# Low parts of streamed weights: a negated write on ScalarE and an accumulating DMA in place of a subtraction on VectorE

## The chip, the cores and the metric

The kernel runs on one core of one Trainium2 chip. The core has a matrix engine (TensorE, PE in the profile), a vector engine (VectorE, DVE), a scalar engine (ScalarE, ACT), GpSimd (POOL), a queue engine that issues DMAs (SyncE, SP), and 16 DMA engines that all queues share. The metric is the device time of one execution in microseconds. Two runs of the kernel before took 730.09 and 731.26 us; the median is 730.67 us.

## The reference

One layer of a diffusion backbone on 512 latent tokens and 256 context tokens, width 1024, all in float32. What is computed, cut to the core:

```python
h  = _rmsnorm(x, pre_g) * (1.0 + sc) + sh           # modulated by silu(c) @ w_mod
hc = _rmsnorm(ctx, pre_g) * (1.0 + sc_c) + sh_c
b_gate, c_gate, x_in, z_a, q, k, v, z_b, g_a, g_b = _split_in(h @ w_in)   # ten blocks of 1024
q, k = _apply_rope(q), _apply_rope(k)
k_c, v_c = jnp.split(hc @ w_in[:, K_OFF:V_END], 2, axis=-1)
attn = _neighbourhood_attention(q, k, v, k_c, v_c, rpb)   # 8 x 16 window + all context keys, 16 heads
y_a = (jax.nn.silu(z_a) * b_gate * _dwconv3(c_gate * x_in, conv_w, conv_b)) @ w_out_conv
y_b = (jax.nn.silu(z_b) * attn) @ w_out_attn
merged = jax.nn.sigmoid(g_a) * y_a + jax.nn.sigmoid(g_b) * y_b
out = x + gt * _rmsnorm(merged @ w_o, post_g)
```

## The kernel before

**Products in three passes.** The matrix engine is used with the type fp32r, which keeps fewer digits than float32. To come close to float32, every operand X is kept as two tiles: a high part H, which is X rounded to fp32r, and a low part L = X - H. A product of weights w and moving data m is then the sum of three matmuls: w.H m.H, w.H m.L and w.L m.H (`step_T`, lines 112 to 117, in this order for every k). A low part is made by `split` (lines 67 to 76): ScalarE copies the source into H (line 70), VectorE subtracts H from the source (line 71).

**Streamed weights.** Most weights of `w_in` and both output weights pass through SBUF in chunks of 1 MB: 128 partitions x 8 k-blocks x 256 columns. `Chunk.__init__` allocates two raw tiles of 4 k-blocks each and has SP load them (line 84), 512 KB each. `Chunk.split` allocates one tile `w` that holds H and L of all 8 k-blocks side by side (in each k-block 256 columns of H, then 256 of L) and splits one half after the other. Raw tiles have 2 buffers, `w` has 2. So the raw load of a chunk can go out when the split of the chunk before has read its raw tiles, and the split of chunk n+1 can begin when PE has finished with chunk n-1, that is, when it begins chunk n. There are 45 streamed chunks. `Chunks` (lines 96 to 110) hands them out in the order of the list `order` and starts the load and split of the next one at each call.

**Stages.** The opening (to about 52 us) normalises x, computes the modulation on VectorE from `w_mod`, and multiplies the first three chunks' worth of weights in an order written out by hand (`manual_schedule` over PE, DVE, ACT and SP; GpSimd isn't among them). The first streamed chunk, `order[3]`, is loaded and split within it (lines 407 and 411). From about 52 to 107 us PE works on the last convolution units of the opening and on channels 2 and 3, chunk after chunk, while VectorE and ScalarE modulate the context tokens (`modulate_c`, which loads `w_mod` slabs through the same SP queue, lines 251 and 451). From 107 to 137 us come the first keys and queries and the first values. From 137 to 512 us attention runs in 64 blocks, with projections of the remaining chunks placed between them by the list `plan`; a block's softmax goes from PE through DVE, ACT, DVE, to PE's transposes, is split into TH and TL (lines 580 to 586) and multiplied with the values in `gather` (line 600). From 512 to 656 us the merge stage takes the output weights and the last gates, chunk after chunk (line 711 on). The end multiplies by `w_o`, whose weights are split by `load_wo` and not by `Chunk`.

**Order of the work.** Each engine runs its own list of instructions in order. In the opening the lists follow the program text. Elsewhere the framework's planner orders them when the kernel is built, by priority in program order and by the costs that it assumes; all semaphores come from the framework as well. PE's list follows the text closely, those of ACT and DVE are interleaved more.

**Where values are used.** In the projections with tokens moving (`unit`, lines 229 to 232) PE first needs a low part of a chunk at its third matmul, and the second half's at k = 4. In `proj_N` (line 128, for the values) one matmul streams H and L together, so the low part is needed at the first.

Of the kernel before, what the change touches and what calls it, by code (L numbers as in the profile page):

```python
# [12 lines left out]
ALU = mybir.AluOpType  # L13
# [14 lines left out]
def layer(ctx: ExitStack, tc, xp, ctxt, ctxT, cc, wmod, small, wfirst, win, wout, wo, rel, tab, out):  # L28
    nc = tc.nc
# [7 lines left out]
    class Banks:  # L37


        def __init__(self, *tags):  # L40
            self.tags, self.n = tags, 0
# [25 lines left out]
    def split(H, L, src, scale=None):  # L67

        if scale is None:
            nc.scalar.copy(H, src)  # L70
            nc.vector.tensor_sub(L, src, H.bitcast(F32))  # L71
        else:
            nc.scalar.mul(H, src, scale)
            nc.vector.scalar_tensor_tensor(
                out=L, in0=src, scalar=scale, in1=H.bitcast(F32), op0=ALU.mult, op1=ALU.subtract
            )

    class Chunk:


        def __init__(self, src):
            self.raws = [wp.tile([P, 4, 256], F32, name="raw", bufs=2) for _ in range(2)]
            for i, raw in enumerate(self.raws):
                nc.sync.dma_start(raw, src[:, 4 * i:4 * i + 4])

        def split(self):
            both = wp.tile([P, KT, 2, 256], F32R, name="w", bufs=2)
            for i, raw in enumerate(self.raws):
                s = slice(4 * i, 4 * i + 4)
                split(both[:, s, 0], both[:, s, 1], raw)  # L90
            return both[:, :, 0], both[:, :, 1], both

    def load_chunk(src):
# [141 lines left out]
    with ExitStack() as p0:  # L235
# [31 lines left out]
        def modulate(k, v, m, H, L):  # L267
            col = cols.pop((k, v))
            nc.scalar.activation(m, m, AF.Identity, bias=col[:, 1:2], scale=col[:, 0:1])
            split(H, L, m)  # L270
# [44 lines left out]
        with tc.manual_schedule(engines={E.PE, E.DVE, E.Activation, E.SP}):  # L315
# [74 lines left out]
            for k in range(KT):  # L390
                cast_first(k)
                condition(k, 0, [1])
                col = cols.pop((k, 0))
                nc.vector.tensor_mul(col[:, 0:1], col[:, 0:1], sp[:, PG + k:PG + k + 1])
                rest_first(k)
                if k == KT - 1:
                    nc.vector.tensor_scalar(out=hcv, in0=sp[:, CW:CW + 32], scalar1=0.5, scalar2=None, op0=ALU.mult)
                if k + 1 < KT:
                    condition(k + 1, 0, [0])
                m = st.tile([P, S], F32, name="m", bufs=2)  # L400
                nc.scalar.activation(m, turned_x.pop(k), AF.Identity, bias=col[:, 1:2], scale=col[:, 0:1])
                split(hx[0][k], hx[1][k], m)
                if k + 3 < KT:
                    load_slab(k + 3)
                    load_first(k + 3)
                elif k == 5:
                    after = Chunk(order[3])
                steps(k)
                if k + 2 < KT:
                    turned_x[k + 2] = turn_x(k + 2)  # L410
# [83 lines left out]
    def values(g):  # L494
        w = chunk()
        for p in (2 * g, 2 * g + 1):
            V[p] = aw.tile([P, 6, 2, P], F32R, name="V", bufs=3)
        for t in range(6):
            ps = pj()
            n = t % 4  # L500
            proj_N(ps, w, hx if t < 4 else hc, slice(n * P, (n + 1) * P))
            vs = summed(ps)
            for i, p in enumerate((2 * g, 2 * g + 1)):
                src = vs[:, i * P:(i + 1) * P].rearrange("p (h d) -> p h d", h=2)
                split(V[p][:, t, :, 0:64], V[p][:, t, :, 64:P], src)
            if t % 2:
                yield
# [371 lines left out]
```

## Time and profile before

| what | value |
|---|---|
| median of two runs | 730.67 us (730.09 to 731.26) |
| profiled execution, span from first to last instruction | 728.6 us; the page gives no other time for it |
| PE busy, instructions | 717.5 us (98%), 3512 matmuls |
| DVE busy | 515.1 us (71%) |
| ACT busy | 332.0 us (46%) |
| POOL busy | 0.7 us, 6 instructions |
| HBM read, written | 83.93 MB, 2.10 MB |
| mean granted TensorE clock | 0.998 |

Busy time is the share of the span in which an engine executes something; a line number such as L117 is that of the kernel. A group is a set of instructions of one line, engine and operation. A wait is the idle time of an engine together with what ended it. The chain is the work that ended last, followed back from the end. A DMA issue is named by its destination and source, with its queue; "SPq" is SP's queue.

### The profile page before, as it was taken

How to read it: one execution, taken by the hardware profiler on the slowest of the kernel's cores; microseconds unless marked ns; L12 is line 12 of the kernel's file. 1: busy time of each engine (PE TensorE's matmuls, PEld its weight loads, DVE VectorE, ACT ScalarE, POOL GpSimd, SP SyncE). 2: the span in 40 equal slices, each digit the busy share in tenths (PEclk: the TensorE clock that was granted, in tenths of full speed). 3: DMA queues.
4: the chain of work that ended last, by engine and by line, in shares of the span. 5: the costliest groups of instructions: out<-in, count | busy, mean ns of one | idle time of the engine just before them, and what ended most of it. 6: DMA issues, size and time to landing. Idle time of an engine off the chain costs nothing.

```text
span 728.6 us, 9358 instructions
## 1 busy us (share of the span) xinstructions
PE 717.5 (98%) x3512; PEld 602.6 (83%) x3512; DVE 515.1 (71%) x1060; ACT 332.0 (46%) x619; POOL 0.7 (0%) x6
## 2 busy tenths in 40 slices
PE   7999999999999999999999999999999999999996
PEld 4888888888888888888888888888888888888885
DVE  6979989996998968879879779675844324335323
ACT  6564523663464654555536446434823213314221
POOL 0000000000000000000000000000000000000000
PEclk9999999999999999999999999999999999999999
DMA  8985883213212222121322212322133133235402
GB/s 332 406 319 174 301 293 112 86 68 108 69 63 73 72 74 73 58 88 58 116 72 73 73 58 73 98 77 72 58 115 109 65 116 101 73 116 180 166 10 107
DMA packets 25967, 86.63 MB, mean 119 GB/s; under 512 B 3009, under 2 KB 3393, under 8 KB 25922
## 3 DMA queue, kind: packets, MB, share of 16 engines
q1 hardware_dynamic: 25778, 85.84, 34.2%
q8 instruction: 27, 0.44, 0.2%
q10 hardware_dynamic: 144, 0.20, 0.1%
q14 instruction: 18, 0.15, 0.1%
HBM read 83.93 MB, written 2.10 MB: 118 GB/s over the span
## 4 chain that ended last, share of the span: by engine, by line
PE 96%; DMA 1%; DVE 1%; ACT 1%; SPq 0%; issue 0%; DVEq 0%; ACTq 0%
PE ps L117 20%; PE ps L116 20%; PE ps L115 20%; PE ps L128 6%; PE ps L755 6%; PE ps L600 4%; PE ps L584 4%; PE ps L133 3%; PE ps L552 3%; PE ps L141 2%; PE ps L307 2%; PE ps L311 2%; PE ps L308 2%; DMA fraw<-in_wfirst 1%; PE ps L561 1%; PE ps L146 1%
## 5 line engine op out<-in xcount | busy, mean ns | idle before, releaser
L115 PE MATMUL ps<-h,w 128*128 128x512 f32 x528 | 207.5, 393 | 0.0
L117 PE MATMUL ps<-h,w 128*128 128x512 f32 x528 | 206.0, 390 | 0.0
L116 PE MATMUL ps<-h,w 128*128 128x512 f32 x528 | 205.7, 390 | 0.0
L71 DVE TENSOR_TENSOR w<-raw,w 128x1024 fp32r<-128x1024 f32 (+1 forms) x98 | 113.1, 1173 | 60.3 <-ACT w L70 60.1
L70 ACT CAST w<-raw 128x1024 fp32r<-128x1024 f32 (+1 forms) x98 | 97.0, 1016 | 95.2 <-PE ps L117 64.0
L117 PEld LDWEIGHTS ps<-h,w 128*128 128x128 f32 x528 | 99.1, 188 | 20.9
L116 PEld LDWEIGHTS ps<-h,w 128*128 128x128 f32 x528 | 99.2, 188 | 20.3
L115 PEld LDWEIGHTS ps<-h,w 128*128 128x128 f32 x528 | 99.2, 188 | 20.1
L575 ACT ACTIVATE pt<-ps,m 128x512 f32<-128x512 f32 x64 | 44.3, 694 | 60.2 <-DVE m L572 60.2
L568 DVE CUSTOM_DVE_ANT_1 ps<-ps,bt 128x512 f32<-128x512 f32 x56 | 38.6, 700 | 15.1 <-PE ps L552 12.0
L71 DVE TENSOR_TENSOR TL<-ps,TH 128x512 fp32r<-128x512 f32 x64 | 42.7, 679 | 5.2 <-ACT TH L70 5.2
L715 DVE SCALAR_TENSOR_TENSOR g<-g,ps 128x512 f32<-128x512 f32 x16 | 11.0, 686 | 42.4 <-PE ps L117 42.4
L70 ACT CAST TH<-ps 128x512 fp32r<-128x512 f32 x64 | 35.1, 588 | 6.6 <-PE ps L584 6.4
L633 ACT ACTIVATE g<-ps 128x512 f32<-128x512 f32 x16 | 9.6, 598 | 59.6 <-PE ps L117 59.6
L584 PE MATMUL ps<-ident,pt 128*128 128x128 f32 x256 | 33.3, 272 | 0.0
L128 PE MATMUL ps<-w,h 128*128 128x512 f32 x128 | 32.7, 395 | 0.0
L577 DVE TENSOR_SCALAR pt<-pt,z 128x512 f32<-128x512 f32 x64 | 30.8, 482 | 1.0
L584 PEld LDWEIGHTS ps<-ident,pt 128*128 128x128 f32 x256 | 29.4, 140 | 2.3
L600 PE MATMUL ps<-TH,V 128*128 128x256 f32 (+1 forms) x96 | 28.5, 319 | 0.0
L600 PE MATMUL ps<-TL,V 128*128 128x256 f32 (+1 forms) x96 | 27.7, 318 | 0.0
L128 PEld LDWEIGHTS ps<-w,h 128*128 128x128 f32 x128 | 23.1, 189 | 4.3
L517 ACT ACTIVATE qd<-ta 64x512 fp32r<-64x512 f32 x32 | 20.2, 631 | 13.5 <-PE ps L561 6.8
(158 smaller groups left out, 1134.9 us busy)
## 6 DMA issues: line engine op xcount, KB each, us to landing
raw<-in_win SPq DMA_DIRECT2D x74, 512.0 KB, 4.2
wm<-in_wmod SPq DMA_DIRECT2D x34, 512.0 KB, 7.2
raw<-in_wout SPq DMA_DIRECT2D x16, 512.0 KB, 4.1
bt<-in_rel SPq DMA_DIRECT2D x16, 256.0 KB, 2.6
raw<-in_wo SPq DMA_DIRECT2D x8, 512.0 KB, 4.2
fraw<-in_wfirst SPq DMA_DIRECT2D x8, 384.0 KB, 8.4
x<-in_xp SPq DMA_DIRECT2D x4, 512.0 KB, 5.4
xr<-in_xp SPq DMA_DIRECT2D x4, 512.0 KB, 5.9
```

The lines of the kernel that those rows point to most:

```text
L70: nc.scalar.copy(H, src)
L71: nc.vector.tensor_sub(L, src, H.bitcast(F32))
L115: nc.tensor.matmul(ps, lhsT=H[:, k, cs], rhs=mH[k], start=k == 0, stop=False)
L116: nc.tensor.matmul(ps, lhsT=H[:, k, cs], rhs=mL[k], start=False, stop=False)
L117: nc.tensor.matmul(ps, lhsT=L[:, k, cs], rhs=mH[k], start=False, stop=k == KT - 1)
L128: nc.tensor.matmul(ps, lhsT=mH[k][:, ts], rhs=both[:, k].rearrange("p a c -> p (a c)"), start=k == 0, stop=False, skip_group_check=True,)
L568: nc.vector.tensor_tensor_reduce(out=s3, in0=s3, in1=bt[:, e::4 - e][:, 0:2], scale=1.0, scalar=-3.0e38, op0=ALU.add, op1=ALU.max, accum_o ...
L575: nc.scalar.activation(pt, s, AF.Exp, bias=m, scale=1.0, accum_out=z)
L577: nc.vector.tensor_scalar(out=pt, in0=pt, scalar1=z, scalar2=None, op0=ALU.mult)
L584: nc.tensor.transpose(tp[:, c], pt[:, c * P:(c + 1) * P], ident)
L600: nc.tensor.matmul(o3[:, dst], lhsT=V[p][:, kt, h], rhs=src(t), start=n == 0 and t is TH, stop=n == len(work) - 1 and t is TL,)
L755: nc.tensor.matmul(ps, lhsT=mm[m][k][:, ts], rhs=w[k][:, cols], start=k + o == 0, stop=k == KT - 1 and o == 2)
```

## The change

Only `Chunk` is changed. For each half of a chunk ScalarE makes H as before, then writes the rounded weights a second time, negated, to the place of L: the product of the raw tile and -1, rounded to the type of the tile, is -H. Then a DMA issued by GpSimd reads the same raw weights once more from HBM and adds them to what lies there, so that the place holds raw - H. It has to wait for the negated write, and PE has to wait for it. VectorE has no part in it any more. The raw tiles are now read by ScalarE alone, twice. `split` itself stays for all other tiles (tokens, softmax tiles, values, merged data, `w_o`).

```diff
@@ -79,6 +79,7 @@
         def __init__(self, src):
+            self.src = src
             self.raws = [wp.tile([P, 4, 256], F32, name="raw", bufs=2) for _ in range(2)]
             for i, raw in enumerate(self.raws):
                 nc.sync.dma_start(raw, src[:, 4 * i:4 * i + 4])
@@ -87,7 +88,9 @@
             both = wp.tile([P, KT, 2, 256], F32R, name="w", bufs=2)
             for i, raw in enumerate(self.raws):
                 s = slice(4 * i, 4 * i + 4)
-                split(both[:, s, 0], both[:, s, 1], raw)
+                nc.scalar.copy(both[:, s, 0], raw)
+                nc.scalar.mul(both[:, s, 1], raw, -1.0)
+                nc.gpsimd.dma_start(both[:, s, 1], self.src[:, s], accum_op=ALU.add)
             return both[:, :, 0], both[:, :, 1], both
```

## The prediction

> **What bounds the kernel now.** I read the page's busy times and its chain first, then the waits of PE alone.
>
> ```profile
> PE 717.5 (98%) x3512; PEld 602.6 (83%) x3512; DVE 515.1 (71%) x1060; ACT 332.0 (46%) x619; POOL 0.7 (0%) x6
> ...
> PE 96%; DMA 1%; DVE 1%; ACT 1%; SPq 0%; issue 0%; DVEq 0%; ACTq 0%
> ```
>
> ```profile
> core 0 of [0], span 728.6 us
> engine line waited for: us in total, times, longest us
> PE ps L355 <- ACT crow L327: 3.3, 1, 3.3
> PE ps L307 <- ACT h L70: 1.1, 1, 1.1
> PE ps L552 <- ACT pt L575: 0.4, 1, 0.4
> ```
>
> PE is busy for 717.5 us of 728.6 and makes up 96% of the chain. A busy PE could still hide stalls, so the second view decides: PE waited three times, 4.8 us together, and the two longest come before any streamed weight is used (L355 and L307 belong to the opening). Whatever the change takes from VectorE, PE has at most 4.8 us to give back. The question is only whether the new way of making the low parts keeps PE free of waits.
>
> The profiled execution has a span of 728.6 us, 2.1 below the median of 730.67; I sum against the span and add 2.1.
>
> **What is removed and added.** A chunk is 1 MB of raw weights in two halves; 45 chunks make 90 halves.
>
> ```profile
> L70 ACT CAST w<-raw x98: 614/1051/1071, 45.1 to 687.6; 128x1024 fp32r<-128x1024 f32 x90, 128x512 fp32r<-128x512 f32 x8
> L71 DVE TENSOR_TENSOR w<-raw,w x98: 683/1217/1226, 46.1 to 688.4; 128x1024 fp32r<-128x1024 f32 x90, 128x512 fp32r<-128x512 f32 x8
> ```
>
> Removed: 90 subtractions of 1.217 us, 109.5 us of DVE, none of it on the path. Worth to the sum: 0.
>
> Added on ACT: 90 negated writes. The trace has none of them; the cast of the same shape, 1.051 us, is the nearest row, so 94.6 us, ACT from 332 to about 427 us of 728.6. Added on GpSimd: 90 accumulating DMAs, each waiting for its negated write. Nothing else is queued behind that wait: POOL has 6 instructions and 0.7 us in all. Added on the DMA engines: 90 x 0.524 MB = 47.2 MB.
>
> ```profile
> q1 hardware_dynamic: 25778, 85.84, 34.2%
> ...
> raw<-in_win SPq DMA_DIRECT2D x74, 512.0 KB, 4.2
> ```
>
> ```profile
> DMA to landing us min/median/max: 3.2/4.1/9.5
> ```
>
> The queue moved 85.84 MB in 34.2% of 728.6 us, which is 249 us, or 1.52 us of all 16 engines for a half. From issue to landing the same half took 3.2 to 9.5 us, 4.1 in the median. No accumulating DMA is in this trace. Below, it can't beat the fastest plain half, 3.2 us. Above, I take two passes (it fetches the old value as well as the weight) of the slowest, 19 us. My value d starts from the median, since most chunks are loaded at a light DMA load: 4.1, plus 1.5 for a second pass, plus some 1 for an issue by GpSimd (an SP issue holds SP 0.33 us in a row below), plus 1.5 for one half of the next chunk's raw load, which starts at the same moment. That is d = 8 us beside other traffic.
>
> The Trainium skill, Collectives: The Full Stack, section "The bandwidth ceiling: the fold count and why AG ≠ RS ≠ AR", says that an adding DMA is half as fast because it "needs two source reads" through one ring; this speaks against the change and for two passes, and no row here shows it. The Trainium skill, DMA: Bandwidth & Descriptors, section "Anatomy of one DMA — SWDGE (gpsimd) path", gives 2.0 us plus bytes over 436 GB/s for one DMA from GpSimd; by that a half takes an estimated 3.2 us and the sum below would be that of the first rival.
>
> **The cover in the dense stretches.** Where chunk follows chunk (two conv channels before attention, the merge stage after it) each lasts 10.9 us on PE, and the two w buffers let chunk n+1 be prepared only while chunk n is multiplied. One merge chunk, from ACT, PE and SP:
>
> ```profile
> 557.98 2.01 ACT L70 CAST w<-raw 128x1024 fp32r<-128x1024 f32 x2 [8.40 <-PE ps L117]
> ...
> 568.66 0.39 PE L115 MATMUL ps<-us,w 128*128 128x512 f32 x1
> 568.88 0.39 PE L116 MATMUL ps<-us,w 128*128 128x512 f32 x1
> 569.11 0.39 PE L117 MATMUL ps<-us,w 128*128 128x512 f32 x1
> ...
> 571.83 0.39 PE L117 MATMUL ps<-us,w 128*128 128x512 f32 x1
> ...
> 560.55 1.47 SPq L84 DMA_DIRECT2D raw<-in_win  x2
> ```
>
> ACT starts the moment the buffer is free (it had waited 8.40 us for PE) and two casts take 2.01 us. With the change cast and negated write of the first half end at +2.0, those of the second at +4.0. PE first needs a low part at its third matmul, 569.11, +11.1; the second half's at k = 4, 571.83, +13.9. So d may be 9.1 us for the first half and 9.9 for the second. At d = 8 no matmul waits, with 1.1 us to spare. The merge stage adds 0, but the cover is thin: each microsecond of d above 9.1 is paid by each dense chunk.
>
> The raw buffers come free on ACT instead of DVE. SP's issues of L84 now wait mostly for the subtraction:
>
> ```profile
> SPq L84 <- DVE w L71: 329.8, 75, 14.3
> ```
>
> ACT's second write ends at +2.0, the first subtraction could not end before 1.05 + 1.22 = 2.3, so the loads go out no later; 0. On ACT the new writes wait for nothing new, the cast ahead of them has waited already.
>
> **DMA load by stage.**
>
> ```profile
> 65.00:115.00 50.00, 50.00 (x222) 41.37 (x221) 46.19 (x75) 20.17 (x35) 0.00 (x0) 1.00 0.71 247
> 115.00:137.00 22.00, 22.00 (x123) 19.19 (x122) 20.98 (x40) 9.43 (x20) 0.00 (x0) 1.00 0.33 110
> 137.00:512.00 375.00, 374.59 (x1959) 320.03 (x1958) 302.83 (x719) 192.52 (x396) 0.00 (x0) 1.00 0.23 76
> 512.00:656.00 144.00, 144.00 (x643) 119.20 (x642) 60.32 (x74) 46.37 (x66) 0.00 (x0) 1.00 0.29 95
> ```
>
> The columns after the stretch are its length, the busy time of PE, PEld, DVE, ACT and POOL, the granted clock (1.00 throughout, so nothing to gain there), the DMA share and GB/s. Two passes for two halves are 6.1 us of DMA per chunk. In the merge 6.1 of 10.9 is 0.56; with 0.29 that is 0.85 and still fits. Between 65 and 115 the share is 0.71, 35.5 us; four to five chunks add 27 and make 63 in 50. The 13 us too many may run into the next stretch, which has 22 x 0.67 = 14.7 us free, as far as its loads aren't urgent: 0 to 13 us of waiting, I take 6.
>
> The first streamed chunk and the first one of attention, with the weights' last load in that stretch:
>
> ```profile
> 45.07 2.00 ACT L70 CAST w<-raw 128x1024 fp32r<-128x1024 f32 x2
> ...
> 52.40 0.39 PE L117 MATMUL ps<-h,w 128*128 128x512 f32 x1
> ...
> 98.27 0.33 SPq L84 DMA_DIRECT2D raw<-in_win  x1
> ...
> 104.84 1.05 ACT L70 CAST w<-raw 128x1024 fp32r<-128x1024 f32 x1 [1.57 <-DMA raw<-in_win]
> ...
> 107.30 0.39 PE L117 MATMUL ps<-h,w 128*128 128x512 f32 x1
> ```
>
> For the first, the negated write ends at 47.1, and with d = 8 the half lands at 55.1, 2.7 us after 52.40; the second half shares the engines and costs about 1.3 more: 4 us. The later one already got its weights late, at 104.84, with PE at its third matmul at 107.30: it is where most of the 6 us will sit. Early stages together: 10 us.
>
> **Attention.** Chunks are 16 us apart and more there, so d isn't critical. ACT is at 192.52 of 375 us and gets 2.1 us more in one go per chunk. Where that falls ahead of the last transposed softmax tile, the gather waits, for its cover is small:
>
> ```profile
> 207.57 0.68 DVE L71 TENSOR_TENSOR TL<-ps,TH 128x512 fp32r<-128x512 f32 x1
> ...
> 208.31 0.40 PE L600 MATMUL ps<-TH,V 128*128 128x512 f32 x1
> ```
>
> The tile was ready at 208.25, 0.06 us ahead. There are 16 gathers. All hit in full would be 34 us; none, 0, since DVE, which comes after ACT in this path, loses 2.4 us per chunk. Near the low end, because PE waited for none of them so far: 3 us.
>
> **Sum.** 728.6 + 10 + 3 + 0 = 741.6, and 2.1 around the span: 743 us, 1.7% above the median. As 2% (14.6 us: 716 and 745) is about what a measurement here can tell, this case lies in "no change" for its larger part.
>
> **The rivals.**
>
> First, everything is covered: an accumulate costs hardly more than a plain half (4 to 5 us). Then only the first chunk is late, by 0 to 2 us, and the time is 731 to 736. For it: the light share of 0.23 to 0.29 after 115 us. Against it: the old value must be fetched too. Chance 0.20.
>
> Second, slower: the accumulate outlasts the dense cover. It decides from d = 9.1 us. At 12 us each of 13 merge chunks that follow one another waits 2.9 us, 38 together, and the four before attention 12 on top of the 13 above: 743 + 50 = 793; at 10 us it is 743 + 0.9 x 17 = 758. For it: a margin of 1.1 us on an estimate whose parts are 4.1 + 1.5 + 1 + 1.5, and plain halves that took up to 9.5. Against it: the median of 4.1. Chance 0.26. Its far end: if GpSimd or the DMA engines hold a chunk for 16 us, every dense chunk pays 5 us, 17 x 5 = 85 us and more, about 830. The trace shows no GpSimd DMA to judge by. Chance 0.07.
>
> Third, the relief of DVE pays: at most 4.8 us, so not 2%. A gain of 2% needs something that no row shows: 0.02.
>
> **How the numbers follow.** The forecast has 0.45 and its own range is 736 to 752, of which about a third lies above 745: 0.16 slower, 0.29 no change. With the rivals: no change 0.29 + 0.20 = 0.49; slower 0.16 + 0.26 + 0.07 = 0.49; faster 0.02. The range runs from the first rival's low end, 731, to the second's at 12 us, 790; left out are the far end (0.07), what of the second lies above (0.06) and below (0.04).
>
> **What would show it.** Right: PE's waits now name the accumulating DMA, some 10 us in all before 115 us and nearly none in the merge; DVE near 406 us, ACT near 427, a new queue with 47 MB; accumulates landing in about 8 us. The first rival: no such waits. The second: waits of like size at every chunk of the merge, and chunks there over 10.9 us apart. Wrong altogether: a landing far from 8 us, negated writes far from 1.05 us, or a changed order of PE's work, since ACT and DVE are ordered by a planner that sees other costs.

## The result and the profile after

The changed kernel is slower: 768.01 us in the median of two runs (764.8 and 771.22) against 730.67; the ratio is 1.052 with a 95% interval from 1.041 to 1.062. Its profiled execution has a span of 763.0 us, 34.4 more than that of before. Lines of the file have moved: L115 to L117 are now L118 to L120, the cast is L91, the negated write L92, the accumulating DMA L93.

The page's busy times, queues, chain and DMA issues:

```profile
PE 727.9 (95%) x3512; PEld 604.8 (79%) x3512; DVE 422.1 (55%) x970; ACT 414.1 (54%) x709; POOL 116.9 (15%) x96
...
q0 software_dynamic: 47520, 47.19, 40.1%
q1 hardware_dynamic: 25778, 85.84, 35.8%
...
PE 71%; DMA 17%; ACT 7%; issue 2%; DVE 2%; POOL 1%; DVEq 0%; SPq 0%; ACTq 0%; POOLq 0%
...
raw<-in_win SPq DMA_DIRECT2D x74, 512.0 KB, 6.4
w<-in_win POOLq DMA_DIRECT2D x74, 512.0 KB, 9.5
...
raw<-in_wout SPq DMA_DIRECT2D x16, 512.0 KB, 7.0
w<-in_wout POOLq DMA_DIRECT2D x16, 512.0 KB, 9.0
```

DVE's busy time fell by 93 us and ACT's rose by 82. The forecast had 109.5 and 94.6, from the lengths of single instructions; instructions that follow one another overlap in the trace (two casts of 1.05 us took 2.01), and the busy time counts the overlap once. The new queue q0 moves 47.19 MB, and its packets take more time in all than those of q1 for 85.84 MB. DMA has gone from 1% to 17% of the chain. PE's waits:

```profile
PE ps L120 <- DMA w<-in_win: 21.1, 13, 5.5
PE ps L358 <- ACT crow L330: 3.2, 1, 3.2
PE ps L120 <- DMA w<-in_wout: 2.6, 1, 2.6
PE ps L310 <- ACT h L70: 1.0, 1, 1.0
PE ps L555 <- ACT pt L578: 0.3, 1, 0.3
```

The two lines of L120 are new; L120 is the matmul that reads the low part. The landing of the halves that GpSimd issues, from the view of the w tile, and the same stretches as in the prediction:

```profile
DMA to landing us min/median/max: 6.6/9.5/19.2
```

```profile
50.00:65.00 15.00, 9.46 (x32) 7.27 (x31) 13.73 (x28) 11.26 (x17) 2.56 (x2) 0.77 1.11 268
65.00:115.00 50.00, 41.70 (x167) 33.22 (x167) 28.86 (x50) 22.21 (x38) 7.70 (x6) 0.93 1.05 297
115.00:137.00 22.00, 20.90 (x91) 16.36 (x90) 14.08 (x28) 8.29 (x9) 5.13 (x4) 1.00 0.97 228
137.00:512.00 375.00, 374.52 (x1965) 320.15 (x1964) 260.57 (x669) 233.97 (x443) 58.95 (x46) 1.00 0.68 137
512.00:656.00 144.00, 139.44 (x628) 113.59 (x627) 37.01 (x70) 72.19 (x99) 30.20 (x24) 1.00 0.89 175
```

PE's busy time (the second number) falls short in the first three stretches and in the last, not in attention. The DMA share (last but one) is 1.05 to 1.11 up to 115 us, 0.89 in the merge; it is the summed time of all packets, so it can pass 1 when packets overlap. The granted clock before it is 0.77 and 0.93 in the first two stretches, where it was 1.00.

Since the stretches shift as PE falls behind, I also measured the stages by PE's own work: from the first matmul of the first streamed chunk to that of the second keys and queries (early), from there to that of the first output weights (attention), and on to the last matmul of those weights (merge). In us, from the starts of these matmuls in each trace, the loss against before in brackets:

| kernel | early | attention | merge | span |
|---|---|---|---|---|
| before | 86.3 | 387.0 | 153.0 | 728.6 |
| changed | 108.6 (+22.3) | 387.3 (+0.4) | 164.9 (+11.9) | 763.0 |
| VectorE adds | 87.3 (+1.0) | 387.0 | 153.0 | 729.7 |
| plain copy | 100.5 (+14.2) | 386.8 | 153.0 (0) | 742.8 |
| 4 KB pieces | 103.6 (+17.3) | 386.8 | 163.9 (+10.9) | 756.4 |
| attention only | 86.3 (0) | 388.5 (+1.5) | 153.0 | 729.6 |
| merge only | 86.3 | 387.0 | 165.2 (+12.3) | 740.9 |
| early only | 110.4 (+24.1) | 387.0 | 153.0 | 752.5 |
| early only, no slab loads | 101.3 (+15.0) | 386.9 | 153.0 | 742.8 |
| early only, no slab loads, halves | 95.0 (+8.7) | 387.0 | 153.0 | 736.4 |
| half tiles | 107.9 (+21.7) | 390.5 (+3.5) | 155.7 (+2.7) | 756.4 |
| late chunks, halves | 86.3 (0) | 387.8 (+0.9) | 154.3 (+1.3) | 730.5 |

The end after the merge takes 50.2 to 50.8 us in all. Kernels with accumulates scatter more between executions than before does, and a profile is one of them; where profile and times disagree, it is said below.

### The profile page after: what moved, and what is told of

Its sections match the earlier page's. It is cut to its first block, busy times and chain, and to the rows that moved or that the text cites. A ratio compares the mean times of both kernels' runs of the same rounds, so it can differ in the third digit from the quotient of the medians.

```text
span 763.0 us, 9519 instructions
## 1 busy us (share of the span) xinstructions
PE 727.9 (95%) x3512; PEld 604.8 (79%) x3512; DVE 422.1 (55%) x970; ACT 414.1 (54%) x709; POOL 116.9 (15%) x96
## 3 DMA queue, kind: packets, MB, share of 16 engines
q0 software_dynamic: 47520, 47.19, 40.1%
q1 hardware_dynamic: 25778, 85.84, 35.8%
## 4 chain that ended last, share of the span: by engine, by line
PE 71%; DMA 17%; ACT 7%; issue 2%; DVE 2%; POOL 1%; DVEq 0%; SPq 0%; ACTq 0%; POOLq 0%
DMA w<-in_win 15%; PE ps L120 14%; PE ps L119 13%; PE ps L118 13%; PE ps L131 6%; PE ps L758 6%; PE ps L603 4%; PE ps L587 3%; PE ps L136 3%; PE ps L555 3%; ACT w L91 2%; ACT w L92 2%; PE ps L144 1%; DMA w<-in_wout 1%; PE ps L310 1%
## 5 line engine op out<-in xcount | busy, mean ns | idle before, releaser
L120 PE MATMUL ps<-h,w 128*128 128x512 f32 x528 | 210.2, 398 | 21.3 <-DMA w<-in_win 21.1
L118 PE MATMUL ps<-h,w 128*128 128x512 f32 x528 | 209.8, 397 | 0.0
L119 PE MATMUL ps<-h,w 128*128 128x512 f32 x528 | 207.9, 394 | 0.0
L93 POOL DMA_DIRECT2D w<-in_win x74 | 95.7, 1293 | 503.3 <-ACT w L92 475.7
L120 PEld LDWEIGHTS ps<-h,w 128*128 128x128 f32 x528 | 100.4, 190 | 49.2 <-DMA w<-in_win 28.3
L91 ACT CAST w<-raw 128x1024 fp32r<-128x1024 f32 x90 | 94.1, 1046 | 57.2 <-PE ps L120 57.0
L119 PEld LDWEIGHTS ps<-h,w 128*128 128x128 f32 x528 | 100.6, 191 | 21.0
L118 PEld LDWEIGHTS ps<-h,w 128*128 128x128 f32 x528 | 100.5, 190 | 20.1
L92 ACT ACTIVATE w<-raw 128x1024 fp32r<-128x1024 f32 x90 | 95.5, 1061 | 0.2
L636 ACT ACTIVATE g<-ps 128x512 f32<-128x512 f32 x16 | 9.6, 598 | 54.2 <-PE ps L120 54.2
L93 POOL DMA_DIRECT2D w<-in_wout x16 | 20.6, 1285 | 73.0 <-ACT w L92 73.0
L520 ACT ACTIVATE qd<-ta 64x512 fp32r<-64x512 f32 x32 | 20.2, 631 | 16.7 <-DVE ta L494 8.3
```

What stands on the lines that cost most here:

```text
L91: nc.scalar.copy(both[:, s, 0], raw)
L92: nc.scalar.mul(both[:, s, 1], raw, -1.0)
L93: nc.gpsimd.dma_start(both[:, s, 1], self.src[:, s], accum_op=ALU.add)
L118: nc.tensor.matmul(ps, lhsT=H[:, k, cs], rhs=mH[k], start=k == 0, stop=False)
L119: nc.tensor.matmul(ps, lhsT=H[:, k, cs], rhs=mL[k], start=False, stop=False)
L120: nc.tensor.matmul(ps, lhsT=L[:, k, cs], rhs=mH[k], start=False, stop=k == KT - 1)
```

## The experiments

Each was timed beside the kernel before on the same chip (medians of before: 730.07, 729.98 and 729.81 us in the three groups).

**ScalarE's part alone.**

```diff
-                nc.gpsimd.dma_start(both[:, s, 1], self.src[:, s], accum_op=ALU.add)
+                nc.vector.tensor_add(both[:, s, 1], both[:, s, 1].bitcast(F32), raw)
```

> The negated write on ScalarE stays, but VectorE adds the raw tile to it, so there is no DMA of GpSimd. Result as in the reference. Theory (the landing of the accumulating DMA is what PE waits for): nothing lands late, PE's waits fall to about those of before (5 us in all), 729 to 734 us. Rival (ScalarE's doubled work delays the weights or the softmax): 745 us or more, PE waits for weights in the merge stage.

730.56 us, ratio 1.0007 (0.9997 to 1.0017). PE's waits, with ACT at 415.0 us:

```profile
PE ps L358 <- ACT crow L330: 3.5, 1, 3.5
PE ps L310 <- ACT h L70: 1.2, 1, 1.2
PE ps L555 <- ACT pt L578: 0.4, 1, 0.4
PE ps L120 <- DVE w L93: 0.3, 1, 0.3
```

The 90 negated writes cost nothing that can be measured (by the interval at most 1.2 us). What costs is the DMA.

**One pass in place of two.**

```diff
-                nc.gpsimd.dma_start(both[:, s, 1], self.src[:, s], accum_op=ALU.add)
+                nc.gpsimd.dma_start(both[:, s, 1], self.src[:, s])
```

> The DMA of GpSimd copies the raw weights over the negated ones and adds nothing: the low part is left out and the raw weights stand in its place. Same issue by GpSimd, same 1 KB pieces, same bytes from HBM, one pass in place of two. Theory (the second pass makes it dear): the queue of GpSimd takes 1.5 to 1.9 us of all engines per half (3.4 with the accumulate), landing 5 to 6.5 us, 733 to 742 us. Rival (issue by GpSimd or the 1 KB pieces make it dear): 3 us or more per half, landing over 8.5 us, over 755 us.

746.04 us, ratio 1.022 (1.020 to 1.025). From its page and the view of the w tile:

```profile
q0 software_dynamic: 47520, 47.19, 25.5%
...
L93 POOL DMA_DIRECT2D w<-in_win x74 | 55.7, 753 | 527.8 <-ACT w L92 495.7
```

```profile
DMA to landing us min/median/max: 4.9/6.6/15.2
```

The same number of packets and bytes take 25.5% of 742.8 us, 2.10 us of all engines per half, against 40.1% of 763.0 us, 3.40 us, with the accumulate. The median landing falls from 9.5 to 6.6 us, and the merge stage loses nothing. So the merge pays for the adding, not for the issue by GpSimd or the 1 KB pieces as such. Some 0.5 of the 2.9 us may lie in GpSimd's own instruction, which takes 1.29 us in the mean with the add and 0.75 without. The early stage still loses 14.2 us: there, plain loads of this size are too much already. All three figures lie between the two expectations, nearer to the theory's: 2.10 us against at most 1.9, 6.6 against 6.5, and the time because both stages were taken together.

**Larger pieces.** The accumulate writes L in four pieces of 1 KB per partition; 47520 packets are 528 per DMA. Here all H stand ahead of all L (the indices that follow from it are left out):

```diff
-            both = wp.tile([P, KT, 2, 256], F32R, name="w", bufs=2)
+            both = wp.tile([P, 2, KT, 256], F32R, name="w", bufs=2)
...
```

> The w tile holds all high parts and then all low parts, so that the accumulate writes 4 KB per partition in one piece and not four pieces of 1 KB. Theory (two passes, whatever the pieces): 3 us or more of all engines per half, landing 8.5 us or more, 757 to 768 us. Rival (small pieces): at most 2.2 us per half, landing about 7 us, 735 to 750 us.

758.77 us, ratio 1.039 (1.037 to 1.041).

```profile
q0 software_dynamic: 12960, 47.19, 32.9%
```

```profile
DMA to landing us min/median/max: 6.6/8.7/11.4
```

With 144 packets per DMA a half takes 2.77 us of all engines (32.9% of 756.4 us over 90), a fifth less than 3.40, and lands 0.8 us earlier in the median. Landing and time are the theory's, the packet time lies between the two expectations: the pieces are a part of the price, and the merge stage still loses 10.9 us.

**Stage by stage.** The accumulate in some chunks, subtraction in the others; `n` numbers the streamed chunks. Against the kernel before, for attention (for the merge the condition is `self.n > 30`, for the early stage `self.n < 7`; the counting is left out):

```diff
-                split(both[:, s, 0], both[:, s, 1], raw)
+                if 7 <= self.n <= 30:
+                    nc.scalar.copy(both[:, s, 0], raw)
+                    nc.scalar.mul(both[:, s, 1], raw, -1.0)
+                    nc.gpsimd.dma_start(both[:, s, 1], self.src[:, s], accum_op=ALU.add)
+                else:
+                    split(both[:, s, 0], both[:, s, 1], raw)
```

> Only the 24 chunks that are prepared in the attention stage are made with the accumulate, all others by subtraction as before. Theory (it costs only where a chunk's cover is short): 729 to 735 us, PE hardly waits in attention. Rival (the accumulate costs wherever it is, by ScalarE's work or DMA contention): 24 of 45 chunks, so about half of the 36 us, 745 us or more.

> Only the 14 chunks from the first of the output weights on are made with the accumulate. Theory (each stage pays for its own late landings): the 11.9 us that the merge stage lost in the changed kernel, so 741 to 744 us. Rival (the merge stage pays for what the early stages upset): 735 us or less.

> Only the first seven streamed chunks, up to the first values, are made with the accumulate. Theory (each stage pays for its own): the 22.3 us of the changed kernel up to 160 us, so 750 to 755 us. Rival (the early waits come from accumulates of later chunks, which share the DMA engines): 742 us or less.

731.40 us, ratio 1.0015 (1.0006 to 1.0024), for attention; 746.69 us, 1.022 (1.019 to 1.025), for the merge; 755.96 us, 1.036 (1.033 to 1.038), for the early stage. Landings in attention, in the merge, early:

```profile
DMA to landing us min/median/max: 6.8/9.5/10.9
```

```profile
DMA to landing us min/median/max: 7.9/10.0/11.9
```

```profile
DMA to landing us min/median/max: 8.8/12.4/19.5
```

24 chunks with a landing of 9.5 us cost 1.3 us in all; there the casts of one chunk after another start 16 us apart in the mean, 11.7 at the least. 14 chunks with 10.0 us cost 16.7 by the times and 12.3 in the profiled execution of 742.65 us; the expected 741 to 744 us holds that execution and not the median (see Scatter at the end). The seven early ones cost 26.0, 1 us above the expected range. The three sum to 44 us by the times and to 37.9 by the profiles, against 37.3 and 34.6 for all together; the stages don't pay for one another, as no stage without accumulates lost anything.

**More cover, same work.** Each half gets a w tile of its own (the tiles of `w_o` that share its name are cut in two as well; these lines and the indices are left out):

```diff
-            both = wp.tile([P, KT, 2, 256], F32R, name="w", bufs=2)
+            both = [wp.tile([P, 4, 2, 256], F32R, name="w", bufs=4) for _ in self.raws]
...
```

> All chunks with the accumulate, but each half of a chunk has a w tile of its own (4 buffers of half the size). The first half's buffer comes free after k = 3 of the second unit, 12 matmuls or 2.7 us before the chunk's end. Theory (PE waits because the landing outlasts its cover): the merge stage loses 2 us or less in place of 11.9, the early stages some of their 22; 750 to 757 us. Rival (the DMA engines can't carry more per chunk in the merge stage, whatever the cover): it still loses 8 us or more, 760 us or more.

758.37 us, ratio 1.038 (1.036 to 1.041). In the merge the loss falls from 11.9 to 2.7 us (the theory had 2 or less), nearly all of it at the second of the 14 chunks, though the landing is still 9.3 us in the median and the DMA share the same:

```profile
512.00:656.00 144.00, 141.86 (x646) 117.24 (x645) 38.22 (x75) 73.67 (x99) 32.03 (x25) 1.00 0.89 177
```

So the engines have room in the merge; it was the cover that was too short. In the early stage (21.7 us) the cover hardly helps. The time is 1.4 us above the expected range, since attention lost 3.5 us, for a reason that stays open, and the early stage almost nothing less.

**The early stage with less to load.** As "early only", and the context modulation and the gains read slabs that are already there:

```diff
             if k < 5:
-                load_slab(k)
+                for j in (8 + k, k):
+                    slabs[j] = slabs[j - k + 5 + k % 3]
...
-            t = st.tile([P, D], F32, name="wm", bufs=6)
-            nc.sync.dma_start(t, wmod[16 + k])
+            t = slabs[5 + k % 3]
```

> As the one before, and 18 loads of modulation weights (9.4 MB, some 27 us of all DMA engines) are left out between 50 and 110 us: the context modulation and the output gains reuse slabs that are already there, so those values are not the reference's. Theory (in the early stages the DMA engines are full, and that makes the landings late): the early loss falls from 22 to 10 us or less, 733 to 741 us. Rival (the accumulate's own time is too long for the cover, full engines or not): it stays at 17 us or more, 747 us or more.

> Accumulates in the first seven streamed chunks alone, the 18 slab loads left out again (context modulation and output gains are not the reference's), and w tiles by halves. Theory (what stayed of the early loss without the slab loads, 15 us, is landings of 9 to 11 us against a cover of 9, plus the first chunk): the cover of 2.7 us more leaves the first chunk's wait of some 7 us, 733 to 737 us. Rival (the rest is not a matter of cover): 13 us or more stay, 739 us or more.

740.60 us, ratio 1.014 (1.013 to 1.016), and with tiles by halves 740.02 us, 1.015 (1.013 to 1.016). Without the slab loads:

```profile
DMA to landing us min/median/max: 8.6/10.0/12.4
```

```profile
65.00:115.00 50.00, 47.60 (x203) 38.74 (x202) 36.93 (x65) 26.11 (x42) 10.26 (x8) 0.97 0.79 159
```

The share falls from 1.02 (early only) to 0.79, the landing from 12.4 to 10.0 us, the time by 15.4 us of the 26.0. Full DMA engines are thus the larger part of the early loss. With the halves neither expectation is met in full: the time is the rival's, above the theory's 737 us, but the loss of some 10 us is below the rival's 13. By the profiles the halves lower the loss from 15.0 to 8.7 us, by the times (10.6 and 10.2) hardly at all. The granted clock makes most of this difference: without the halves the profiled execution has 0.50 from 57.3 to 62.1 us and from 96.4 to 99.7, which costs half of that time, 4.1 us; with them it has 1.00 there. Its mean clock is 0.998, but 0.993 in the other three executions with halves. In the two traces PE's waits in this stage (9.9 and 7.5 us) and the clock (4.1 and 0) leave only about 1 us of the loss open. Why these waits stay, those of the first chunk (5.2 and 3.3 us) among them, was not tested further.

**Accumulates where they are covered.** Subtraction in the first seven chunks, accumulates by halves in all later ones (`self.n > 6` with the half tiles).

> Subtraction on VectorE in the first seven streamed chunks, accumulates in all later ones, w tiles by halves; result as in the reference. Theory (a stage costs nothing where the landing is covered and the DMA engines have room): 728.6 us of span plus the 3.5 and 2.7 us that attention and merge lost with half tiles, 733 to 737 us. Rival (half tiles only moved the loss): 741 us or more, with waits in the merge stage.

735.08 us, ratio 1.007 (1.005 to 1.008). PE waits for the accumulates no longer than this:

```profile
PE ps L128 <- DMA w<-in_win: 1.1, 2, 0.9
```

Of the 45 chunks 38 are made with the accumulate, and the loss is 5 us where it was 37. It is still no gain, since PE was busy for 98% of the span before. Of these 5 us the profiled execution, 732.45 us, shows 2. A third w buffer, 16 KB more per partition, might give more cover; it wasn't tried.

## Why the prediction was right or wrong

The range of 731 to 790 us holds the time, but the likeliest case, 743 us and "no change", isn't what came. The second rival did: the accumulate outlasts the dense cover. I had given it 0.26. The range reaches from the first rival to the second, so that the time lies in it says little for the working.

- **Right: nothing to gain from VectorE.** PE had 4.8 us to give. In the plain copy VectorE is relieved as well and PE doesn't wait in the merge, which takes 153.0 us as before; with the accumulates only in attention the time is 1.3 us above before.
- **Right: the negated writes.** 1.057 us in the median against the cast's 1.051, and hidden, as ScalarE's part alone shows.
- **Right as a measure, wrong as a price: the cover.** That PE would wait where d passes some 9 us is right. That "each microsecond of d above 9.1 is paid by each dense chunk" is not: in the changed kernel every second chunk of the merge waited. The end of one chunk that doesn't and the start of one that does, from ACT, POOL and PE:

```profile
571.34 0.60 ACT L636 ACTIVATE g<-ps 128x512 f32<-128x512 f32 x1 [4.84 <-PE ps L120]
571.84 1.04 ACT L91 CAST w<-raw 128x1024 fp32r<-128x1024 f32 x1
572.78 1.06 ACT L92 ACTIVATE w<-raw 128x1024 fp32r<-128x1024 f32 x1
...
582.27 1.05 ACT L91 CAST w<-raw 128x1024 fp32r<-128x1024 f32 x1 [6.54 <-PE ps L120]
...
574.13 1.28 POOL L93 DMA_DIRECT2D w<-in_win  x1 [9.75 <-ACT w L92]
...
571.14 0.39 PE L118 MATMUL ps<-us,w 128*128 128x512 f32 x1
...
571.60 0.39 PE L120 MATMUL ps<-us,w 128*128 128x512 f32 x1
...
582.02 0.39 PE L118 MATMUL ps<-h,w 128*128 128x512 f32 x1
582.25 0.39 PE L119 MATMUL ps<-h,w 128*128 128x512 f32 x1
583.45 0.50 PE L120 MATMUL ps<-h,w 128*128 128x512 f32 x1 [0.81 <-DMA w<-in_win]
```

The chunk that starts at 571.14 reaches its third matmul, 571.60, without a wait. The next one's would be due at 582.48 and starts at 583.45. Its negated write ended 2.0 us after its cast began, as forecast, at 573.84; so its cover was 8.6 us and d, from there to 583.45, 9.6. The cover is below 9.1 because a gate's activation (L636) stood ahead of the cast. Before, every second chunk had that too: the cast of 569.35 begins 0.7 us after the first matmul of its chunk on PE at 568.66, that of the forecast's row, 557.98, 0.2 us after the like matmul at 557.78. And the cast for the chunk behind it begins at 582.27, before PE waits: a wait lengthens the next chunk's cover. The runs don't part these two reasons. In the merge-only trace 9 of 13 chunks waited, again not each.

So the second rival's price at d = 10, 0.9 us for each of 13 chunks or 12 us, meets the measured 11.9 us by luck: 7 chunks waited and lost 1.7 us each in the mean, the second halves' waits included.

- **Wrong, mis-sized: "plus 1.5 for a second pass".** The parts of d for one pass, 4.1 + 1 + 1.5, sum to what the plain copy measured, 6.6 us; that each part is right is not shown. The adding adds 2.9 us to that, not 1.5, for 9.5 in all, and a half with it takes 3.40 us of all engines, not 2 x 1.52. The forecast d = 8 was 1.5 us too short, more than the 1.1 us that I had to spare, and the merge's 0 became 11.9.

The Trainium skill, Collectives: The Full Stack, section "The bandwidth ceiling: the fold count and why AG ≠ RS ≠ AR", has the adding step of a collective at half the speed of the copying one, for its two reads; here the ratio of the packet times in the same pieces is 3.40 to 2.10, 1.6. The Trainium skill, DMA: Bandwidth & Descriptors, section "Anatomy of one DMA — SWDGE (gpsimd) path", gave an estimated 3.2 us for a half; the fastest plain half from GpSimd took 4.9 us here, and the measurement decides.

- **Wrong, mis-sized: the early stage, 10 us, measured 22.3.** I saw that 63 us of DMA were wanted in 50 and assumed that the 13 too many would mostly be put off ("I take 6") at a landing of 8. In the early-only kernel, with a share of 1.02 to 1.11 up to 115 us, the landings were 8.8 to 19.5 us. Taking 9.4 MB of other loads away gave back 15.4 us. The three longest waits of PE in the changed kernel:

```profile
57.47 0.79 PE L120 MATMUL ps<-h,w 128*128 128x512 f32 x1 [5.54 <-DMA w<-in_win]
...
89.51 0.80 PE L120 MATMUL ps<-h,w 128*128 128x512 f32 x1 [3.83 <-DMA w<-in_win]
...
106.31 0.57 PE L120 MATMUL ps<-h,w 128*128 128x512 f32 x1 [4.01 <-DMA w<-in_win]
```

The first chunk waited 5.5 us, where I had 2.7 + 1.3. The rest did not sit mostly at the first chunk of attention (1.1 us), but at the second halves of the third and fourth streamed chunk, 3.8 and 4.0 us, whose accumulates took 14.3 and 19.2 us to land. All waits of the stage are some 15 us. A further loss of about 5.6 us was in no step: PE's clock (below).
- **About right: attention.** 3 us forecast, 0.4 measured. The gathers were not delayed by ACT. The reading behind it was off, though: chunks are not "16 us apart and more" there, but 11 to 22, 16 in the mean.
- **A small slip: the raw loads.** The reading "the loads go out no later" looked at the first half alone. In the merge SP's two issues ended 4.2 and 4.8 us after the cast began in two chunks of the changed kernel, 4.0 in a chunk before; nothing waited for it there, as ACT's casts waited for PE.
- **Right: the order of PE's work** didn't turn: all but 7 of its 3512 matmuls stand in the same place.

## What to carry to other kernels

Where TensorE never waits, work taken off another engine is worth nothing, and the question for the new path is its latency against the time for which a buffer is free: write that cover down for each kind of chunk (here 9.1 and 8.6 us), follow a wait into the next chunk, whose cover it lengthens, and trust a forecast only if the margin is larger than the uncertainty of the longest unmeasured term. A DMA that adds to what lies in SBUF took 1.6 times the packet time of a copy of the same pieces here, and it lands late where the engines are full already; put it only where the cover is long. When a wait of a few microseconds can't be removed, splitting the buffer so that its first half comes free earlier can hide it without more memory (11.9 to 2.7 us in the merge).

## What the runs showed of the hardware

**A wait can also slow what follows it.** After three waits of PE, of 5.5 us and about 4 us twice, the granted clock is 0.50 for a few microseconds. The changed kernel, in and right after two of these stretches (count of matmuls in brackets, clock third from the end):

```profile
57.50:62.20 4.70, 4.70 (x11) 3.73 (x12) 4.70 (x9) 3.79 (x6) 2.56 (x2) 0.50 1.14 268
62.30:67.00 4.70, 4.70 (x22) 3.89 (x21) 2.21 (x6) 0.00 (x0) 0.00 (x0) 1.00 1.10 276
89.60:92.90 3.30, 3.30 (x8) 2.62 (x9) 3.30 (x9) 1.30 (x3) 0.00 (x0) 0.50 1.11 329
93.00:96.30 3.30, 3.30 (x16) 2.68 (x15) 0.85 (x2) 0.00 (x0) 0.00 (x0) 1.00 1.11 326
```

PE counts as fully busy in all four but does half the matmuls in the first and third: half of 4.7, 3.3 and, at 106.7, another 3.3 us is lost, about 5.6 us in all, which no wait shows. The length of the wait alone doesn't decide: a wait of 2.4 us was followed by 0.50 in the early kernel without slab loads, waits of 2.6 us (the merge's longest here) and 3.3 us (the first chunk without slab loads, by halves) were not. What else decides was not tested. The Trainium skill, TensorE: Matmul & The Clock Gate, section "Part 1: The HAM clock gate (the "warmup" mystery)", says that about 3.4 us without matmuls bring the array to half its clock. The changed kernel's three waits, 3.8 to 5.5 us, agree; the 2.4 us of the other kernel is less, and there the measurement decides.

**Even the fastest accumulate is long.** The fastest accumulate took 6.6 us to land, the fastest plain copy from GpSimd 4.9, the fastest plain load from SP 3.2. In pieces of 4 KB the fastest accumulate took 6.6 us too, though its packets take a fifth less time.

**Scatter.** In the three groups of experiments before lies within 729.6 and 730.5 us; the kernels with many accumulates spread over 2 to 6 us (764.8 to 771.2, 742.7 to 748.1). The mean granted clock goes with it in most of them. In merge only, the profiled execution took 742.65 us at 0.997, the others 745.51, 748.07 and 747.87 us at 0.993, 0.993 and 0.991. A mean lower by 0.004 to 0.006 is 3.0 to 4.5 us of 745, and they are 2.9 to 5.4 us longer. As only merge chunks are changed there, their waits seem to lower the clock in some executions; none of these was profiled. The clock is not all: in the kernel of the last experiment 732.45, 734.58 and 735.58 us all have 0.998.
